# Last MLP of a hybrid attention block: its first two feature groups by pairs of row tiles

## The chip, the cores and the metric

The kernel runs on one core of a Trainium2 chip. The core has five engines that work side by side: TensorE (PE in the profile, its weight loads as PEld), VectorE (DVE), ScalarE (ACT), GpSimd (POOL) and SyncE (SP), which here only issues transfers. Each engine takes its own instructions strictly in the order in which they stand in its list and waits on semaphores for the others. Matmuls write to PSUM, everything else lives in SBUF, and inputs, outputs and some intermediate tensors in DRAM. The metric is the time of one launch in device microseconds.

## The reference

One transformer block over 1024 positions of width 1024 (float32): a hybrid attention, an attention to a memory of 256 rows, and an MLP with squared ReLU, each with a norm ahead and a residual add behind.

```python
x = x + hybrid_mixer(rms_norm(x, norm1_g), ...)          # sparse attention, 8 + 8 heads, @ w_out
x = x + memory_xattn(rms_norm(x, norm2_g), mem, ...)     # w_xq, 4 heads of 128 over 256 rows, @ w_xo
x = x + square(relu(rms_norm(x, norm3_g) @ w_ff_in)) @ w_ff_out   # 1024 -> 4096 -> 1024
```

## The kernel before

The 1024 rows are eight tiles of 128 (numbered 0 to 7). The kernel first projects all rows and runs the hybrid attention tile by tile. Beside the attention it runs a "filler": for tiles 0 to 3 the out projection, memory attention and whole MLP, then the out projection and memory attention of tiles 4 and 5. When the attention is over there remain the end of that filler, the same for tiles 6 and 7, and the MLP of tiles 4 to 7. This last part, from some 1330 us on, is what the change touches.

`between(pool, t0, nt, x2s, keep)` (L902) does the out projection and the memory attention for `nt` tiles from `t0`: it loads the attention outputs `o` (L908) and the residual `x` (L912), multiplies by `w_out` (fp32 matmuls of 256 columns, two TensorE passes each), adds to the residual (`add_to`, L899), norms (`norm_T2`, L290), multiplies by `w_xq`, and does one item of memory attention for each pair of heads and each tile (L939 to L986): scores, exponentials, transposes of the probabilities (L972), values; its output goes through DRAM (`xo`, written at L986, read at L992), is transposed and multiplied by `w_xo`. The result x2 stays in SBUF (`keep`) or goes to DRAM (L1000).

`mlp(pool, t0, nt, x2s)` (L1002) does the MLP of four tiles. It loads the x2 that are not in SBUF (L1007), norms and transposes all four tiles (each into a high and a low part, `xh` and `xl`, of fp32r type), then goes through eight groups of 512 features. In a group, four "feature" accumulations of 24 matmuls each (8 slices of k, times high-high, low-high, high-low) make 128 features for 512 rows: the weights are the stationary side, the 512 rows move. ScalarE takes relu and square (L1034, L1035), POOL splits the result into `h` parts (L1037, L1038). Then eight "down" accumulations (four tiles by two column halves) of 12 matmuls of 512 columns use the features as stationary side and `w_ff_out` as moving side; the DVE adds each to x2 (L899).

Every weight piece of 128 x 512 elements is loaded into `wraw` and split into a high and a low part (`split_w`, L240): the high part by ScalarE (L244), the low part by DVE or POOL (L249), as the list `plan["w"]` says in turn. `PLAN_TAIL` is ("ag", "av", "ag"): high always on ScalarE, low two times of three on POOL.

The order on each engine is not written out by hand. The program is traced in Python order (`merge` interleaves two generators by the weights they yield), and a planner then orders the instructions of each engine by the traced priority and by when, in its own model, their inputs and their buffers are ready. So work that is traced later is put into gaps where its inputs are there. A pool's tag is a ring of as many buffers as `RINGS` gives; a tile waits until the old user of its place is done. Transfers are issued in order by SP, and those of the memory's keys and values (L929, L930) by POOL.

The lines that set up the last part:

```python
merge((rest, REST), (between(d2, 6, 2, x2s, True), 45.0))
dn_pool.__exit__(None, None, None)
drain(mlp(d2, 4, 4, x2s))
```

`rest` is the remaining filler (memory attention of tiles 4 and 5, in pool `dn`); `d2` is the pool of the last part.

Of the kernel before, what the change touches and what calls it, by code (L numbers as in the profile page):

```python
# [10 lines left out]
F32R = mybir.dt.float32r  # L11
# [11 lines left out]
P = 128  # L23
L = 1024
DM = 1024
# [7 lines left out]
NCMP = 63  # L33
KG = 2
NS = 4
RINGS = {
    "p1": {"x4": 5, "st": 2, "relu": 4, "wraw": 4, "whi": 6, "wlo": 6, "c8": 4, "c4": 2, "kraw": 5, "pc": 2},
    "p2": {"x4": 3, "st": 1, "relu": 2, "whi": 4, "wlo": 4, "c8": 3, "c4": 1, "kraw": 4, "pc": 2},
    "dn": {"b4": 4, "h": 8, "relu": 2, "wraw": 2, "whi": 4, "wlo": 4},
    "d2": {"b4": 4, "h": 8, "relu": 2, "wraw": 3, "whi": 6, "wlo": 6},  # L40
}
PSUMS = {"p1": {"D": 4, "M": 3, "C": 1}, "main": {"S": 2, "PT": 2, "PV": 1, "D": 2, "M": 1}}
TAGS = {"p1": ("D", "M", "C"), "p2": ("D", "M", "D"), "dn": ("D", "M"), "d2": ("S", "PT")}
PLAN_HEAD = ("ag", "av")
PLAN_MAIN = ("ag",)
PLAN_TAIL = ("ag", "av", "ag")

SLC, WIN, DSA, IDX = 0, 2, 4, 5

# [34 lines left out]
def drain(gen):  # L84
    for _ in gen:
        pass
# [19 lines left out]
def merge(a, b):  # L106
    drain(beside(*a, *b))
# [59 lines left out]
def build(nc, tc, I, C, out):  # L167
# [72 lines left out]
    def split_w(raw, hi, lo):  # L240
        h, l = plan["w"][plan["i"] % len(plan["w"])]
        plan["i"] += 1
        if h == "a":
            s.activation(hi, raw, AF.Copy)  # L244
# [4 lines left out]
        (v if l == "v" else g).tensor_tensor(lo, raw, hi, op=ALU.subtract)  # L249
# [78 lines left out]
    def xT(pool, nt, whole=False):  # L328

        parts = [pool.tile([P, DM // P, nt * P], F32 if whole else F32R, tag="x" + n, name="x" + n)  # L330
                 for n in ("h" if whole else "hl")]
        return (parts, [lambda t, k, x=x: x[:, k, t * P:(t + 1) * P] for x in parts],
                lambda t: [x[:, :, t * P:(t + 1) * P] for x in parts])
# [565 lines left out]
            v.tensor_tensor(dst, pt, dst, op=ALU.add)  # L899
        return add_to  # L900

    def between(pool, t0, nt, x2s, keep):  # L902

        o_of = []
        for t in range(nt):
# [1 line left out]
            for c in range(8):  # L907
                nc.sync.dma_start(o[:, c, :], oT_dr[t0 + t][c])  # L908
            o_of.append(o)
        x2 = [ring(pool, "b4", [P, DM]) for t in range(nt)]  # L910
        for t in range(nt):
            nc.sync.dma_start(x2[t], I["x"][0, (t0 + t) * P:(t0 + t + 1) * P, :])  # L912
        add_to = residual_add(x2)
# [88 lines left out]
    def mlp(pool, t0, nt, x2s):  # L1002
# [13 lines left out]
        for f4 in range(8):  # L1016
# [24 lines left out]
            for c in range(2):  # L1041
# [4 lines left out]
                for t in range(nt):  # L1046
# [11 lines left out]
                                          x2[t][:, c * 512:(c + 1) * 512])  # L1058
                    yield 2.6

    def pe_stack():
# [68 lines left out]
    ctx.close()  # L1130


# [19 lines left out]
```

## Time and profile before

| | |
|---|---|
| median of 3 runs | 1837.35 us (1835.46 to 1839.35) |
| the profiled execution's own time | 1835.75 us |
| its span, first to last instruction | 1833.9 us |
| mean granted TensorE clock | 0.970 |
| TensorE busy | 1726.9 us (94%) |
| DVE, ACT, POOL busy | 936.1, 1074.6, 895.0 us |

The profile is of one execution. "Busy" is time in instructions of that engine. "Idle before" is an engine's waiting time just ahead of a group of instructions, with the engine or transfer that ended it. The granted clock is the share of full speed at which TensorE was let run. The chain is the sequence of work that ended last, followed back from the last instruction. A matmul's length in the profile includes its way through the pipeline, so the distance between the starts of two matmuls in a row is what one costs.

### The profile page before, as it was taken

Reading aid. Unit: us, or ns where it says so; the run is one execution under the profiler, and the core shown is the slowest. Engines: PE = TensorE matmul, PEld = TensorE weight load, DVE = VectorE, ACT = ScalarE, POOL = GpSimd, SP = SyncE. Lnnn points to the kernel's source line nnn. Section 1 sums busy time; section 2 is a strip of 40 time slices with the busy share of each in tenths; the row PEclk is TensorE's granted clock in tenths of the full one; section 3 lists DMA queues with packets and bytes.
Section 4 is the critical chain, followed back from the end, with each engine's and each line's share of the span. In section 5 each row is a group of like instructions: output and inputs, shape, how many; then the busy total and the mean of one; then the engine's idle time right before and its main releaser. Section 6 shows DMA issues by size and latency. Waiting matters only on the chain. (4 is left out here: it accounts for less than half of the span.)

```text
span 1833.9 us, 28049 instructions
## 1 busy us (share of the span) xinstructions
PE 1726.9 (94%) x9262; PEld 1474.2 (80%) x9262; DVE 936.1 (51%) x2353; ACT 1074.6 (59%) x2687; POOL 895.0 (49%) x1034
## 2 busy tenths in 40 slices
PE   5996999889989998999999999999999799999999
PEld 5995988777878787778887788888988578787787
DVE  4553766575684678466664656646523422222222
ACT  4444658889588669955797457994412323333332
POOL 2364657446262244677676576662111144454443
PEclk9997998999999999999999999999989799999999
DMA  8224512256335320222112112125394222222232
GB/s 203 70 87 160 103 34 79 78 193 180 122 112 162 120 81 24 73 81 71 64 63 91 54 65 75 60 79 185 99 288 131 71 69 92 92 93 93 94 99 98
DMA packets 180081, 187.50 MB, mean 102 GB/s; under 512 B 34656, under 2 KB 149088, under 8 KB 179936
## 3 DMA queue, kind: packets, MB, share of 16 engines
q1 hardware_dynamic: 172000, 175.23, 30.8%
q0 software_dynamic: 7936, 10.49, 2.2%
q8 instruction: 73, 1.20, 0.3%
q14 instruction: 72, 0.59, 0.1%
HBM read 164.69 MB, written 20.97 MB: 101 GB/s over the span
## 5 line engine op out<-in xcount | busy, mean ns | idle before, releaser
L249 POOL TENSOR_TENSOR wlo<-wraw,whi 128x512 fp32r<-128x512 f32 (+1 forms) x230 | 308.5, 1347 | 278.7 <-ACT whi L244 247.6
L244 ACT ACTIVATE whi<-wraw 128x512 fp32r<-128x512 f32 (+2 forms) x289 | 181.1, 628 | 247.4 <-PE psS L218 147.1
L218 PE MATMUL psD<-whi,xh 128*128 128x256 f32 (+1 forms) x704 | 193.8, 359 | 3.6 <-ACT whi L244 2.9
L218 PE MATMUL psD<-wlo,xh 128*128 128x256 f32 (+1 forms) x704 | 194.8, 357 | 0.8 <-DMA wlo<-in_w_in_dram 0.8
L236 DVE TENSOR_TENSOR pl<-psPT,ph 128x512 fp32r<-128x512 f32 (+1 forms) x232 | 142.2, 621 | 78.2 <-ACT ph L235 75.4
L218 PE MATMUL psD<-whi,h 128*128 128x512 f32 x512 | 174.3, 404 | 1.8 <-POOL h L1037 1.0
L688 ACT ACTIVATE S<-S,mn 128x128 f32<-128x128 f32 (+7 forms) x192 | 142.7, 744 | 41.5 <-DVE mn L686 40.3
L218 PE MATMUL psS<-whi,h 128*128 128x512 f32 x512 | 162.1, 392 | 5.1 <-DVE b L899 5.1
L693 POOL TENSOR_SCALAR S<-S,sums,gi 128x640 f32<-128x640 f32 (+7 forms) x128 | 107.7, 850 | 106.7 <-DVE sums L691 99.0
L235 ACT ACTIVATE ph<-psPT 128x512 fp32r<-128x512 f32 (+1 forms) x232 | 122.8, 540 | 60.9 <-PE psPT L703 54.5
L249 DVE TENSOR_TENSOR wlo<-wraw,whi 128x512 fp32r<-128x512 f32 (+1 forms) x59 | 64.3, 1090 | 166.9 <-ACT whi L244 166.8
L218 PEld LDWEIGHTS psD<-whi,xh 128*128 128x128 f32 x704 | 134.0, 198 | 14.3 <-ACT whi L244 3.3
L218 PEld LDWEIGHTS psD<-wlo,xh 128*128 128x128 f32 x704 | 134.8, 197 | 12.5 <-DMA wlo<-in_w_in_dram 1.2
L703 PE MATMUL psPT<-c_ident,S 128*128 128x128 f32 x816 | 132.3, 279 | 8.3 <-DVE ql L236 4.2
L899 DVE TENSOR_TENSOR b<-psS,b 128x512 f32<-128x512 f32 (+1 forms) x80 | 50.0, 635 | 152.6 <-PE psS L218 152.6
L218 PEld LDWEIGHTS psS<-whi,h 128*128 128x128 f32 x512 | 96.1, 188 | 29.3 <-DVE b L899 9.3
L218 PE MATMUL psS<-K,qh 128*128 128x384 f32 (+3 forms) x288 | 113.5, 397 | 5.6 <-DVE mn L686 2.8
L218 PEld LDWEIGHTS psD<-whi,h 128*128 128x128 f32 x512 | 95.6, 190 | 23.7 <-DVE b L899 1.5
L703 PEld LDWEIGHTS psPT<-c_ident,S 128*128 128x128 f32 x816 | 98.1, 143 | 18.9 <-POOL S L693 5.6
L218 PE MATMUL psD<-wlo,h 128*128 128x512 f32 x256 | 102.5, 404 | 1.3 <-POOL wlo L249 1.3
L218 PE MATMUL psD<-xh,wlo 128*128 128x512 f32 x256 | 101.5, 398 | 0.0
L899 DVE TENSOR_TENSOR b<-psD,b 128x512 f32<-128x512 f32 (+1 forms) x112 | 63.2, 572 | 74.5 <-PE psD L218 73.0
(299 smaller groups left out, 4647.4 us busy)
## 6 DMA issues: line engine op xcount, KB each, us to landing
wraw<-in_w_ff_in_dram SPq DMA_DIRECT2D x128, 256.0 KB, 2.7
wraw<-in_w_ff_out_dram SPq DMA_DIRECT2D x128, 256.0 KB, 2.6
whi<-in_w_out_dram SPq DMA_DIRECT2D x32, 256.0 KB, 5.0
wlo<-in_w_out_dram SPq DMA_DIRECT2D x32, 256.0 KB, 4.6
wraw<-in_w_in_dram SPq DMA_DIRECT2D x24, 256.0 KB, 3.1
q<-st SPq DMA_DIRECT2D x12, 512.0 KB, 2.6
qin<-q SPq DMA_DIRECT2D x44, 128.0 KB, 2.3
x<-in_x_dram SPq DMA_DIRECT2D x8, 512.0 KB, 5.2
```

Of the source, the lines that this page charges most:

```text
L218: te.matmul(o, a, b, start=start, stop=stop)
L235: s.activation(hi, src, AF.Copy)
L236: v.tensor_tensor(lo, src, hi, op=ALU.subtract)
L244: s.activation(hi, raw, AF.Copy)
L249: (v if l == "v" else g).tensor_tensor(lo, raw, hi, op=ALU.subtract)
L688: s.activation(S, S, AF.Exp, bias=low, scale=-1.0, accum_out=sums[:, hh:hh + 1])
L693: g.tensor_scalar(Ss[hh], Ss[hh], sums[:, hh:hh + 1], 1.0 if gate is None else gate[:, hh:hh + 1], op0=ALU.mult, op1=ALU.mult)
L703: te.transpose(p2[:, j, hh, :], S[:, (c + j) * P:(c + j + 1) * P], ident)
L899: v.tensor_tensor(dst, pt, dst, op=ALU.add)
```

## The change

The MLP of tiles 4 to 7 is written anew as `mlp_tail`. Its first `G` = 2 feature groups are done for tiles 4 and 5 alone, ahead (in traced order) of the norms of tiles 6 and 7; groups 2 to 7 are done for all four tiles; groups 0 and 1 for tiles 6 and 7 come last. The weights of groups 0 and 1 are therefore loaded and split twice. A feature accumulation of a pair has 256 rows in place of 512; down matmuls are as before. Weights come in chunks of 512 KB (four k slices of 256 columns, or two rows of 512) in place of 256 KB, and are split piece by piece as before.

The pools change with it. Residuals of the last part have a pool `res` of their own, norm weights a tag `g`, features a ring of 16 in place of 8. `d2` now only serves the memory attention of tiles 6 and 7, with weight rings of 4 in place of 6 and no `wraw`. The new pool `d3` lies on the side of `dn`, opens when `dn` and `d2` are closed, and takes its PSUM tiles from the tags D (two buffers) and M (one) in place of S and PT (two each). `PLAN_TAIL` alternates between POOL and DVE.

```diff
+G = 2
 RINGS = {
     "dn": {"b4": 4, "h": 8, "relu": 2, "wraw": 2, "whi": 4, "wlo": 4},
-    "d2": {"b4": 4, "h": 8, "relu": 2, "wraw": 3, "whi": 6, "wlo": 6},
+    "res": {"b4": 4},
+    "d2": {"b4": 2, "h": 8, "relu": 2, "whi": 4, "wlo": 4},
+    "d3": {"g": 2, "h": 16, "relu": 2, "wraw": 4, "whi": 10, "wlo": 10},
 }
-TAGS = {... "dn": ("D", "M"), "d2": ("S", "PT")}
+TAGS = {... "dn": ("D", "M"), "d2": ("S", "PT"), "d3": ("D", "M")}
-PLAN_TAIL = ("ag", "av", "ag")
+PLAN_TAIL = ("ag", "av")
...
-    def between(pool, t0, nt, x2s, keep):
+    def between(pool, t0, nt, x2s, keep, res=None):
...
-        x2 = [ring(pool, "b4", [P, DM]) for t in range(nt)]
+        x2 = [ring(res or pool, "b4", [P, DM]) for t in range(nt)]
...
+    def mlp_tail(pool, res, x2s, t0):
+        x2 = {}
+        (xh, xl), _, xt_of = xT(pool, 4)
+        gb3 = [ring(pool, "g", [P, 512]) for _ in range(2)]
+        for i, gb in enumerate(gb3):
+            nc.sync.dma_start(gb, row(W["norm3_g"][i * 512:(i + 1) * 512]).to_broadcast([P, 512]))
+
+        def start(t):
+            if t0 + t in x2s:
+                x2[t] = x2s[t0 + t]
+            else:
+                x2[t] = ring(res, "b4", [P, DM])
+                nc.sync.dma_start(x2[t], x2_dr[t0 + t])
+            norm_T2(pool, x2[t], gb3, xt_of(t))
+
+        def features(f4, ts):
+            cols = slice(ts[0] * P, (ts[-1] + 1) * P)
+            for f2 in range(2):
+                gr = []
+                for k0 in range(0, 8, 4):
+                    c0 = (f4 * 4 + f2 * 2) * P
+                    raw = ring(pool, "wraw", [P, 4, 256])
+                    nc.sync.dma_start(raw, W["w_ff_in"][k0 * P:(k0 + 4) * P, c0:c0 + 256]...)
+                    for k in range(0, 4, 2):
+                        hi, lo = ring(pool, "whi", [P, 2, 256], F32R), ring(pool, "wlo", [P, 2, 256], F32R)
+                        split_w(raw[:, k:k + 2, :], hi, lo)
+                        gr += [(hi[:, i, :], lo[:, i, :]) for i in range(2)]
+                for f in range(2):
+                    pt = pst(TAGS[pool.name][0], [P, len(ts) * P])
+                    fs = slice(f * P, (f + 1) * P)
+                    for k in range(8):
+                        wh, wl = gr[k]
+                        mm(pt, wh[:, fs], xh[:, k, cols], k == 0, False)
+                        mm(pt, wl[:, fs], xh[:, k, cols], False, False)
+                        mm(pt, wh[:, fs], xl[:, k, cols], False, k == 7)
+                    yield pt
+
+        def down(pt, hs, ws, us):
+            for f, ((hh, hl), (wh, wl)) in enumerate(zip(hs, ws)):
+                mm(pt, hh[:, us], wh, f == 0, False)
+                mm(pt, hh[:, us], wl, False, False)
+                mm(pt, hl[:, us], wh, False, f == len(hs) - 1)
+
+        def group(f4, ts, last):
+            hs = []
+            for pt in features(f4, ts):
+                n = len(ts) * P
+                r = ring(pool, "relu", [P, n])
+                s.activation(r, pt, AF.Relu)
+                s.activation(r, r, AF.Square)
+                hh, hl = ring(pool, "h", [P, n], F32R), ring(pool, "h", [P, n], F32R)
+                g.tensor_scalar(hh, r, 1.0, 1.0, op0=ALU.mult, op1=ALU.mult)
+                g.tensor_tensor(hl, r, hh, op=ALU.subtract)
+                hs.append((hh, hl))
+            for c in range(2):
+                cs = slice(c * 512, (c + 1) * 512)
+                ws = []
+                for k in range(0, 4, 2):
+                    raw = ring(pool, "wraw", [P, 2, 512])
+                    r0 = (f4 * 4 + k) * P
+                    nc.sync.dma_start(raw, W["w_ff_out"][r0:r0 + 256, cs]...)
+                    for i in range(2):
+                        hi, lo = ring(pool, "whi", [P, 512], F32R), ring(pool, "wlo", [P, 512], F32R)
+                        split_w(raw[:, i, :], hi, lo)
+                        ws.append((hi, lo))
+                for t in ts:
+                    pt = pst(TAGS[pool.name][0], [P, 512])
+                    down(pt, hs, ws, slice((t - ts[0]) * P, (t - ts[0] + 1) * P))
+                    v.tensor_tensor(x2[t][:, cs], pt, x2[t][:, cs], op=ALU.add)
+                    if last:
+                        nc.sync.dma_start(out[0, (t0 + t) * P:(t0 + t + 1) * P, cs], x2[t][:, cs])
+
+        for ts in ((0, 1), (2, 3)):
+            for t in ts:
+                start(t)
+            if ts[0] == 0:
+                for f4 in range(G):
+                    group(f4, ts, False)
+        for f4 in range(G, 8):
+            group(f4, (0, 1, 2, 3), False)
+        for t in (0, 1):
+            nc.sync.dma_start(out[0, (t0 + t) * P:(t0 + t + 1) * P, :], x2[t])
+        for f4 in range(G):
+            group(f4, (2, 3), f4 == G - 1)
...
-    d2_pool = tc.tile_pool(name="d2", bufs=1, side="right", reuse_waits="tile")
+    res_pool = tc.tile_pool(name="res", bufs=1, side="right", reuse_waits="tile")
+    res = res_pool.__enter__()
+    d2_pool = tc.tile_pool(name="d2", bufs=1, side="right", reuse_waits="tile")
...
-    merge((rest, REST), (between(d2, 6, 2, x2s, True), 45.0))
+    merge((rest, REST), (between(d2, 6, 2, x2s, True, res), 45.0))
     dn_pool.__exit__(None, None, None)
-    drain(mlp(d2, 4, 4, x2s))
     d2_pool.__exit__(None, None, None)
+    with tc.tile_pool(name="d3", bufs=1, reuse_waits="tile") as d3:
+        mlp_tail(d3, res, x2s, 4)
+    res_pool.__exit__(None, None, None)
     ctx.close()
```

More of the change, by code (lines that the diff above doesn't have):

```diff
@@ L39 @@
     "dn": {"b4": 4, "h": 8, "relu": 2, "wraw": 2, "whi": 4, "wlo": 4},
-    "d2": {"b4": 4, "h": 8, "relu": 2, "wraw": 3, "whi": 6, "wlo": 6},
+    "res": {"b4": 4},
+    "d2": {"b4": 2, "h": 8, "relu": 2, "whi": 4, "wlo": 4},
+    "d3": {"g": 2, "h": 16, "relu": 2, "wraw": 4, "whi": 10, "wlo": 10},
 }
 PSUMS = {"p1": {"D": 4, "M": 3, "C": 1}, "main": {"S": 2, "PT": 2, "PV": 1, "D": 2, "M": 1}}
-TAGS = {"p1": ("D", "M", "C"), "p2": ("D", "M", "D"), "dn": ("D", "M"), "d2": ("S", "PT")}
+TAGS = {"p1": ("D", "M", "C"), "p2": ("D", "M", "D"), "dn": ("D", "M"), "d2": ("S", "PT"), "d3": ("D", "M")}
 PLAN_HEAD = ("ag", "av")
 PLAN_MAIN = ("ag",)
-PLAN_TAIL = ("ag", "av", "ag")
+PLAN_TAIL = ("ag", "av")
 SLC, WIN, DSA, IDX = 0, 2, 4, 5
@@ L1059, in mlp @@
                     yield 2.6
+    def mlp_tail(pool, res, x2s, t0):
[18 more added lines that the diff above has]
+                    raw = ring(pool, "wraw", [P, 4, 256])
+                    nc.sync.dma_start(raw, W["w_ff_in"][k0 * P:(k0 + 4) * P, c0:c0 + 256].rearrange("(k p) n -> p k n", p=P))
+                    for k in range(0, 4, 2):
[33 more added lines that the diff above has]
+                    r0 = (f4 * 4 + k) * P
+                    nc.sync.dma_start(raw, W["w_ff_out"][r0:r0 + 256, cs].rearrange("(k p) n -> p k n", p=P))
+                    for i in range(2):
[20 more added lines that the diff above has]
+            group(f4, (2, 3), f4 == G - 1)
```

## The prediction

> **What bounds the kernel now.** I read the page's engine line and chain first, then the chain in order of time, then busy time in short windows around the place where the chain begins.
>
> The page, and the start and end of the chain in order of time (start, length, what):
>
> ```profile
> PE 1726.9 (94%) x9262; PEld 1474.2 (80%) x9262; DVE 936.1 (51%) x2353; ACT 1074.6 (59%) x2687; POOL 895.0 (49%) x1034
> PE 19%; DVE 1%; issue 0%
> ...
> 1469.14 28.00 PE psS L218 x119
> ...
> 1497.91 44.12 PE psS L218 x191
> ...
> 1542.05 0.70 DVE b L899
> ...
> 1542.80 44.12 PE psS L218 x191
> ...
> 1830.18 0.69 DVE b L899
> ```
>
> From 1469 us to the end the chain is TensorE alone: the last MLP, eight feature groups, each 1542.80 - 1497.91 = 44.89 us (192 matmuls and one wait of some 0.75 us for the DVE add that frees a PSUM tile). Nothing but fewer or denser TensorE instructions shortens that stretch. Ahead of it TensorE is not dense. Windows (length, then busy us and count of PE, PEld, DVE, ACT, POOL, granted clock, DMA share, GB/s):
>
> ```profile
> 1410.00:1420.00 10.00, 10.00 (x51) 8.91 (x51) 3.03 (x9) 1.15 (x3) 0.71 (x1) 1.00 0.62 199
> 1420.00:1430.00 10.00, 7.89 (x38) 5.91 (x37) 4.95 (x15) 4.92 (x14) 1.98 (x2) 0.78 0.47 157
> 1430.00:1440.00 10.00, 6.30 (x25) 5.39 (x25) 0.85 (x2) 0.60 (x1) 0.00 (x0) 0.50 0.27 80
> 1440.00:1450.00 10.00, 9.31 (x40) 7.69 (x39) 2.30 (x5) 1.86 (x3) 1.29 (x1) 0.86 0.09 26
> 1450.00:1460.00 10.00, 6.99 (x35) 5.53 (x33) 3.46 (x10) 5.14 (x10) 3.77 (x5) 0.99 0.25 79
> 1460.00:1470.00 10.00, 7.41 (x28) 5.36 (x28) 8.72 (x15) 5.06 (x9) 0.95 (x2) 0.50 0.00 0
> ```
>
> Between 1420 and 1470 TensorE works through the serial end of the memory attention of tiles 6 and 7, then the four norms, with gaps and a granted clock down to 0.50. All four norms come before the first feature matmul, so nothing fills these gaps. Its timeline there (start, length, instruction, idle before it and releaser):
>
> ```profile
> 1420.52 0.38 PE L274 MATMUL psPT<-c_ident,relu 128*128 128x128 f32 x2
> ...
> 1436.25 1.09 PE L274 MATMUL psPT<-c_ident,relu 128*128 128x128 f32 x4 [3.01 <-DMA relu<-xo]
> ...
> 1451.22 1.03 PE L218 MATMUL psS<-wlo,xh 128*128 128x256 f32 x4
> 1452.09 1.03 PE L218 MATMUL psS<-whi,xh 128*128 128x256 f32 x4
> ...
> 1458.68 1.34 PE L274 MATMUL psPT<-c_ident,relu 128*128 128x128 f32 x8 [2.98 <-DVE relu L297]
> ...
> 1468.79 0.78 PE L218 MATMUL psS<-xh,whi 128*128 128x512 f32 x1
> ...
> 1514.36 0.39 PE L218 MATMUL psS<-xh,whi 128*128 128x512 f32 x1
> ```
>
> The first feature matmul stands at 1468.79, the second group's first at 1514.36.
>
> **The change, part by part.** In the instruction order of the changed program every engine's list is the old one up to the start of the memory attention of tiles 6 and 7 (some 1330 us here); only what follows moves.
>
> *Feature groups 0 and 1 on tiles 4 and 5 alone.* They need only the norms of 4 and 5, so the planner lays their 2 x 96 feature and 2 x 48 down matmuls between the steps of the attention of 6 and 7, and the norms of 6 and 7 behind group 1. Groups 0 and 1 for tiles 6 and 7 come last. Feature matmuls are cut from 512 columns to 256, twice as many; down matmuls stay 512 wide and equal in number. The width's price is taken from the first projection, same type, same 256 columns:
>
> ```profile
> 30.00 0.28 PE L218 MATMUL psD<-whi,xl 128*128 128x256 f32 x1
> ...
> 31.81 0.28 PE L218 MATMUL psD<-wlo,xh 128*128 128x256 f32 x1
> ...
> 1475.24 0.39 PE L218 MATMUL psS<-xh,whi 128*128 128x512 f32 x1
> ...
> 1477.10 0.40 PE L218 MATMUL psS<-xl,whi 128*128 128x512 f32 x1
> ...
> 1513.46 0.62 PE L218 MATMUL psS<-whi,h 128*128 128x512 f32 x2
> ...
> 1514.14 0.39 PE L218 MATMUL psS<-whi,h 128*128 128x512 f32 x1
> ```
>
> Sixteen starts lie between the first two (all 17 are in the trace at 0.11 to 0.12): 1.81/16 = 0.113 us. At 512 columns the two rows stand eight starts apart: 1.86/8 = 0.232. Half of 0.232 is 0.116, so cutting the width costs nothing here: a pair's group is 96 x 0.114 + 48 x 0.227 (0.68/3) + 0.75 = 22.6 us, two of them 45.2 against 44.89. The wait for the DVE add comes once per pair instead of once per group, which is in the 45.2. The Trainium skill says otherwise (TensorE: Matmul & The Clock Gate, Back-to-back issue gap): pairs of weight load and matmul are said to sustain 81 ns at 128 columns and 131 at 512, which by a straight line, my estimate, puts 256 at three quarters of 512. By that rule the sum would rise by 384 x 0.25 x 0.232 = 22 us; the projection's rows do not agree with it.
>
> *What the filling can win.* In the old program the stretch 1420.5 to 1514.36 (93.9 us) holds group 0 and this work of 6 and 7 and of the norms, at full-clock prices: 64 passes of 0.217 us (0.87/4, above) = 13.9; 24 + 12 small attention matmuls at about 0.12 = 4.3; 52 transposes at about 0.12 = 6.2; together 24.4. With 45.2 for the pair groups that is 69.6: the ceiling of the gain is 93.9 - 69.6 = 24.3 us. The floor is below zero, since in-order queues can also make TensorE wait.
>
> *When the filling can start.* The x2 of tiles 4 and 5 still goes through DRAM. SP issues, and the first work released by the second read:
>
> ```profile
> 1415.13 0.32 SPq L1000 DMA_DIRECT2D x<-b  x1
> 1419.84 0.32 SPq L1007 DMA_DIRECT2D b<-x  x1
> 1422.49 0.69 POOL L231 TENSOR_TENSOR xqr<-xqms,mhalf 128x2 f32<-128x2 f32 x1 [0.38 <-DMA b<-x]
> L293 ACT ACTIVATE xh<-b 128x1024 fp32r<-128x1024 f32 x4 | 4.2, 1047 | 0.3 <-PE psS L218 0.3
> L244 ACT ACTIVATE whi<-wraw 128x512 fp32r<-128x512 f32 x13 | 8.2, 631 | 16.7 <-PE psS L218 16.3 <-issue 0.2
> L235 ACT ACTIVATE xh<-psPT 128x512 fp32r<-128x512 f32 x8 | 4.8, 596 | 5.1 <-PE psPT L274 5.1
> L966 ACT ACTIVATE relu<-psS,xnb,xsc 128x256 f32<-128x256 f32 x4 | 2.2, 562 | 1.4 <-DVE xnb L963 1.4
> L235 ACT ACTIVATE h<-psPT 128x256 fp32r<-128x256 f32 x2 | 0.8, 381 | 1.1 <-PE psPT L274 1.1
> ```
>
> Tile 5 lands at 1422.45. The changed order puts its sum of squares on ScalarE ahead of the query splits of 6 and 7, which now run as soon as their transposes (1420.52) are done: that chain starts late, at 1422.45 + 1.05 and a short read of the sum, about 1423.7. Before the norm of 5 is split (its first half), ScalarE's list holds two query splits, both halves of 4, six weight splits and two exponentials: 2 x 0.38 + 3 x 0.60 + 6 x 0.63 + 2 x 0.56 = 7.5, so 1431.2; with a DVE subtraction, the second half's transposes and handoffs dense features run from about 1434.5. TensorE has 14 us from 1420.5 to there and 4.9 us of work in it (16 norm and 9 other transposes, 12 score matmuls, four features, at 0.12): 9.1 lost. The first weights come late as well: the old program had three chunks loaded long before, now the first load stands behind tile 5's read on SP (1419.84 + 0.32); the read itself took 2.6 us to land, and twice that for the larger chunk still hides behind the same wait.
>
> *Interleaving.* DVE and POOL now split weights (32 pieces for the two pair groups) while the attention of 6 and 7 needs them. Group rows of the dense MLP, and one DVE split with POOL idle:
>
> ```profile
> L249 POOL TENSOR_TENSOR wlo<-wraw,whi 128x512 fp32r<-128x512 f32 x48 | 63.9, 1339 | 83.3 <-ACT whi L244 82.7
> L249 DVE TENSOR_TENSOR wlo<-wraw,whi 128x512 fp32r<-128x512 f32 x24 | 27.2, 1131 | 81.9 <-ACT whi L244 81.9
> 1474.47 0.69 DVE L249 TENSOR_TENSOR wlo<-wraw,whi 128x512 fp32r<-128x512 f32 x1 [3.98 <-ACT whi L244]
> ```
>
> A split takes DVE 1.13 on average against 0.69 alone. I take 3 us for small waits of this kind and 1.5 for the low clock at the start (0.50 in two of the windows). The bounds are 0 and 21: the two returns of the attention output through DRAM, priced below, hidden or bare; 3 is near the lower end since each has some 8 us of matmuls in front. The Trainium skill (SBUF — State Buffer, two separate sides) names an exclusive port pair for which the loser of DVE and POOL waits through the other's whole instruction; the 1.13 agrees, and by it a DVE step of the attention could wait up to a POOL split longer.
>
> *Other queues and pools.* SP loses the three early loads; residuals with their own pool are read before the attention outputs, two issues (0.3 to 0.5 us each) off the way to w_out. The d2 weight rings fall from 6 to 4, so w_out's third chunk waits for its first: at worst a landing (2.6 us, as above) lies bare, though a chunk of w_out is 32 passes, 6.9 us, of cover. I set the two against each other: 0, bounds -1 and +2. At the end each pair group splits its 16 pieces in 22.6 us: on POOL eight low parts, and four feature splits of two 256-wide instructions, each under 1.34: at most 16 x 1.34 = 21.4 us, so it holds. DVE now takes half of the low parts instead of a third: 8 x 1.13 in 44.89, hidden.
>
> **Sum.** 69.6 + 9.1 + 3 + 1.5 puts the end of group 1 and of the attention at 1420.5 + 83.2 = 1503.7 against 1514.36: -10.7. The last two pair groups, 45.2 against 44.89, give +0.3: -10.4. The span of 1833.9 becomes 1823.5, the profiled execution's 1835.75 becomes 1825.3. That execution is 1.6 under the median of 1837.35; against the median I put 1826.9.
>
> **Rivals.**
> *The filling fits without friction.* The attention chain of 6 and 7 would be hidden from 1424 on, and only x2's landing is lost, 4 us: gain 19, time 1817. For it: TensorE is 10.00 busy in the window before 1420, where two such streams are already interleaved. Against: the queue of ScalarE above.
> *The groups do not start early.* The new pool lies over that of tiles 4 and 5 and its tiles wait for the old ones; if these waits, or late weights, hold features until the attention is done (1444 to 1455), most of the gap stays: 1833 to 1837. Against: the loads go out at 1420.
> *SP holds the attention back (slower).* In the new order the write and read of the attention output of tile 6 stand behind the fifth and sixth weight loads, those of tile 7 behind the eighth, and these wait for slots that DVE and POOL free. The return alone costs:
>
> ```profile
> 1433.74 0.42 SPq L986 DMA_DIRECT2D xo<-relu  x1
> 1436.57 0.32 SPq L992 DMA_DIRECT2D relu<-xo  x1
> 1441.60 1.06 PE L274 MATMUL psPT<-c_ident,relu 128*128 128x128 f32 x4
> ```
>
> That is 7.9 us from write to transposes. TensorE is in order: two returns, each with two splits (2 x 1.34) in front, bare, would be 21 us, 18 above what I took, so 1845. The gain is gone once 13.4 of the 21 lie bare. Against: 60 features and 12 small matmuls (8.2 us) stand in front of the first return's transposes, 48 features and nine down matmuls (7.5) in front of the second's.
> *Narrow matmuls cost more.* If 256 columns took 0.217 as the fp32 passes do, 384 x 0.10 = 38 us more, 1865. The projection's rows speak against it. By the Trainium skill's rule above it would be 22 us more.
>
> **How the numbers follow.** The forecast as worked out (1820 to 1833) has 0.55; the frictionless case 0.2; no early start 0.12; SP 0.1; narrow matmuls 0.03. A measurement here tells about 0.2% (3.7 us) from no change. Faster holds the first two, 0.75, and a little of the third: 0.78. Same is most of the third and some of the fourth, 0.11; slower 0.11. The range reaches from the frictionless case and some 3 us past it (the prices at 0.12 are rounded), 1814, into the case without early start, 1836.
>
> **What would show it.** In the changed trace: 256-wide feature matmuls 0.114 apart from about 1434; group 2's first 512-wide one near 1504; six periods of about 44.9 us, then two of about 22.6; TensorE idle of some 9 us between 1420 and 1435 and under 5 us between 1435 and 1500; a granted clock of 1.00 from 1440. It is wrong if TensorE waits for the return of the attention output by more than 10 us, if 256-wide starts are further apart than 0.13, or if the last pair groups wait for weights.

## The result and the profile after

The changed kernel takes 1826.46 us (median of four runs, 1821.91 to 1827.33) against 1837.31 for the kernel before: a ratio of 0.9935, 95% interval 0.9918 to 0.9952, so 9 to 15 us less against a measurement that tells some 4. The prediction was 1826.9. The profiled execution is the fastest of the four (1821.91 us, span 1820.1), while that of before was a middling one. The page of the changed kernel:

```profile
PE 1715.2 (94%) x9454; PEld 1475.6 (81%) x9454; DVE 957.4 (53%) x2390; ACT 1094.6 (60%) x2735; POOL 910.1 (50%) x1045
```

The total hides where the time went, so I cut the span at four instructions that both kernels have, in TensorE's timeline (start, length, instruction, idle before it and releaser). Before:

```profile
1334.99 4.94 PE L218 MATMUL psD<-h 128*128 128x128 f32 x22
...
1785.10 0.39 PE L218 MATMUL psS<-xh,whi 128*128 128x512 f32 x1
...
1829.76 0.39 PE L218 MATMUL psS<-whi,h 128*128 128x512 f32 x1
```

After:

```profile
1330.51 4.11 PE L221 MATMUL psD<-h 128*128 128x128 f32 x22
...
1412.35 0.38 PE L277 MATMUL psPT<-c_ident,relu 128*128 128x128 f32 x2
...
1500.28 0.51 PE L221 MATMUL psD<-xh,whi 128*128 128x512 f32 x1 [0.83 <-ACT xh L238]
...
1768.90 0.28 PE L221 MATMUL psD<-xh,whi 128*128 128x256 f32 x1
...
1815.83 0.39 PE L221 MATMUL psD<-whi,h 128*128 128x512 f32 x1
```

The first row (a values product of the memory attention of tiles 4 and 5) is the last instruction whose whole past on the four computing engines is the same in both programs (SP already issues other transfers before it). The second is the last query transposes of tile 6 (those of tile 7 follow at 1421.99 and 1415.62); the matmul records between the two (430 after, 429 before) are of the same kinds in both programs, in a slightly different order. The third is the first 512-wide feature matmul behind the interleaved stretch (group 2's after, group 1's before), the fourth stands six whole groups later. Before, the second and third are the rows at 1420.52 and 1514.36 of the prediction.

| stage, us | before | after | difference | forecast |
|---|---|---|---|---|
| A: values product to query transposes | 85.53 | 81.84 | -3.69 | 0 |
| B: query transposes to the first 512-wide group | 93.84 | 87.93 | -5.91 | -10.7 |
| C: six whole groups | 270.74 | 268.62 | -2.12 | 0 |
| D: the rest, to the last matmul | 44.66 | 46.93 | +2.27 | +0.3 |
| tail, A to D | 494.77 | 485.32 | -9.45 | -10.4 |

The first row itself stands 4.5 us earlier in the profile after, which the change cannot have done; over all profiled executions below it stands anywhere from 1330.5 to 1336.0. So each kernel below is told by its time and by its tail.

Stage B in windows (length, busy us and count of PE, granted clock, DMA share, GB/s):

```profile
1412.35:1426.59 14.24, 7.63 (x34) 0.67 1.01 332
1426.59:1434.00 7.41, 7.41 (x47) 0.71 0.55 164
1434.00:1484.60 50.60, 50.60 (x317) 1.00 0.44 136
1484.60:1500.28 15.68, 11.05 (x44) 0.78 0.35 112
```

Between 1434 and 1485 the gap is filled: TensorE is busy throughout at full clock. The stage is 87.93 long for the 69.6 of work that the prediction counted, so 18.3 are lost where 13.6 were forecast. With the prediction's prices (estimates, rounded, so that they sum to 19), some 10 go in the first window, 2 in the second to the low clock, and 7 in the last. Of these 7, 4.6 are waits (3.80 and 0.83, below and above); most of the rest is the clock, which is at 0.50 again around the longer wait. TensorE works in 5.31 of these 6.80 us, at half speed, which costs some 2.7:

```profile
1488.90:1495.70 6.80, 5.31 (x15) 0.50 0.38 130
```

The timeline of TensorE in the middle and in the last window:

```profile
1442.06 0.60 PE L277 MATMUL psPT<-c_ident,relu 128*128 128x128 f32 x4
...
1445.98 0.60 PE L277 MATMUL psPT<-c_ident,relu 128*128 128x128 f32 x4
...
1484.61 0.60 PE L277 MATMUL psM<-c_ident,relu 128*128 128x128 f32 x4
...
1490.39 1.09 PE L277 MATMUL psM<-c_ident,relu 128*128 128x128 f32 x4 [3.80 <-DVE xl L239]
```

The first two are the returns of the attention output of tiles 6 and 7 through DRAM: no idle before them, so the feared wait is hidden. The loss of the last window is one that the prediction has no line for: the norm of tile 6 has one PSUM tile (tag M); its second half can be transposed only when the DVE has read the first, and the DVE's list shows why that is late:

```profile
1482.34 2.58 DVE L252 TENSOR_TENSOR wlo<-wraw,whi 128x512 fp32r<-128x512 f32 x2
1485.55 2.43 DVE L300 SCALAR_TENSOR_TENSOR relu<-b,nr,g 128x512 f32<-128x512 f32 x2 [0.63 <-POOL h L1118]
1487.90 1.75 DVE L252 TENSOR_TENSOR wlo<-wraw,whi 128x512 fp32r<-128x512 f32 x1
1489.57 0.68 DVE L239 TENSOR_TENSOR xl<-psM,xh 128x512 fp32r<-128x512 f32 x1
```

The weight split of 1.75 just ahead of the read runs beside one on POOL (1487.34 to 1489.10); alone it takes 0.68 to 0.69 (19 splits of this kernel from 1400 us on that no POOL instruction overlaps).

### The profile page after: what moved, and what is told of

The parts are those of the page before. It is cut to its first block, busy times and chain, and to the rows that moved or that the text cites. A ratio compares the mean times of both kernels' runs of the same rounds, so it can differ in the third digit from the quotient of the medians.

```text
span 1820.1 us, 28417 instructions
## 1 busy us (share of the span) xinstructions
PE 1715.2 (94%) x9454; PEld 1475.6 (81%) x9454; DVE 957.4 (53%) x2390; ACT 1094.6 (60%) x2735; POOL 910.1 (50%) x1045
## 3 DMA queue, kind: packets, MB, share of 16 engines
q8 instruction: 75, 1.23, 0.3%
## 4 chain that ended last, share of the span: by engine, by line
PE 66%; DVE 9%; ACT 8%; POOL 7%; issue 5%; DMA 5%; SPq 0%; POOLq 0%; ACTq 0%; DVEq 0%
PE psD L221 47%; PE psS L221 8%; PE psPV L221 4%; PE psPT L706 4%; ACT dmask L647 2%; POOL wlo L252 2%; PE psM L277 1%; POOL S L696 1%; DMA wraw<-in_w_ff_in_dram 1%; DVE S L689 1%; DVE pl L239 1%; ACT whi L247 1%; ACT ph L238 1%; ACT tkt L649 1%; ACT tks L648 1%
## 5 line engine op out<-in xcount | busy, mean ns | idle before, releaser
L221 PE MATMUL psD<-whi,h 128*128 128x512 f32 x1024 | 340.7, 401 | 7.3 <-DVE b L1134 5.4
L247 ACT ACTIVATE whi<-wraw 128x512 fp32r<-128x512 f32 x321 | 200.7, 628 | 209.9 <-PE psD L221 155.1
L221 PEld LDWEIGHTS psD<-whi,h 128*128 128x128 f32 x1024 | 192.9, 190 | 53.1 <-DVE b L1134 8.8
L221 PE MATMUL psD<-xh,wlo 128*128 128x512 f32 (+1 forms) x576 | 212.7, 370 | 0.0
L221 PE MATMUL psD<-xh,whi 128*128 128x512 f32 (+1 forms) x576 | 211.8, 372 | 0.9 <-ACT xh L238 0.8
L221 PE MATMUL psD<-xl,whi 128*128 128x512 f32 (+1 forms) x576 | 212.2, 370 | 0.0
L221 PE MATMUL psD<-wlo,h 128*128 128x512 f32 x512 | 203.3, 399 | 1.3 <-POOL wlo L252 1.3
L221 PEld LDWEIGHTS psD<-whi,xh 128*128 128x128 f32 x704 | 132.3, 195 | 14.2 <-ACT whi L247 3.4
L221 PEld LDWEIGHTS psD<-xh,whi 128*128 128x128 f32 x576 | 108.8, 189 | 18.6 <-ACT xh L238 1.6
L221 PEld LDWEIGHTS psD<-xh,wlo 128*128 128x128 f32 x576 | 108.9, 189 | 17.1 <-POOL wlo L252 0.3
L221 PEld LDWEIGHTS psD<-xl,whi 128*128 128x128 f32 x576 | 108.8, 189 | 17.1
```

The costliest lines, as they stand in the source:

```text
L221: te.matmul(o, a, b, start=start, stop=stop)
```

## The experiments

Stages of each kernel as above, in us; the kernel before had medians of 1835.4 to 1837.3 in these comparisons.

| kernel | time | ratio to before, 95% | A | B | C | D | tail |
|---|---|---|---|---|---|---|---|
| before | | | 85.5 | 93.8 | 270.7 | 44.7 | 494.8 |
| changed | 1826.5 | 0.9935 (0.9918 to 0.9952) | 81.8 | 87.9 | 268.6 | 46.9 | 485.3 |
| whole groups | 1834.5 | 0.9990 (0.9979 to 1.0002) | 82.6 | 100.2 | 268.0 | 44.5 | 495.3 |
| before, x first | 1836.8 | 1.0005 (0.9993 to 1.0018) | 86.7 | 94.4 | 270.9 | 44.7 | 496.7 |
| before, x first, rings of 4 | 1847.8 | 1.0068 (1.0044 to 1.0092) | 88.6 | 95.9 | 278.2 | 46.5 | 509.2 |
| changed, x late, rings of 6 | 1828.2 | 0.9956 (0.9941 to 0.9970) | 87.9 | 86.8 | 268.5 | 46.9 | 490.2 |
| changed, norms in PT | 1830.7 | 0.9967 (0.9955 to 0.9979) | 82.4 | 96.6 | 268.1 | 46.9 | 494.0 |
| changed, x2 kept | 1825.9 | 0.9939 (0.9927 to 0.9951) | 83.2 | 86.6 | 268.6 | 46.9 | 485.3 |
| changed, low on DVE | 1819.7 | 0.9908 (0.9892 to 0.9925) | 81.6 | 80.9 | 269.0 | 46.1 | 477.6 |
| changed, low on POOL | 1834.2 | 0.9998 (0.9989 to 1.0007) | 81.8 | 90.8 | 269.7 | 54.0 | 496.3 |
| changed, low on DVE, x2 kept | 1813.7 | 0.9878 (0.9859 to 0.9897) | 83.0 | 79.3 | 269.0 | 46.1 | 477.5 |
| changed, three pairs | 1826.8 | 0.9953 (0.9938 to 0.9969) | 82.7 | | | | 489.5 |
| changed, three pairs, low on DVE | 1819.8 | 0.9913 (0.9897 to 0.9929) | 82.6 | | | | 480.5 |
| before, low on DVE | 1834.0 | 0.9992 (0.9979 to 1.0005) | 85.2 | 94.7 | 269.5 | 44.7 | 494.1 |

With x2 kept, the first four norm transposes of tile 4 stand in stage A instead of B.

### Are the pair groups the gain?

```diff
-G = 2
+G = 0
...
-            group(f4, (0, 1, 2, 3), False)
-        for t in (0, 1):
+            group(f4, (0, 1, 2, 3), G == 0 and f4 == 7)
+        for t in (0, 1) if G else ():
```

> The changed kernel with all eight feature groups done for all four tiles (G = 0): pools, PSUM tags, load sizes and the early read of the residual stay as changed, only the pair groups are gone. Theory of the prediction: pools and queues are worth nothing and the pair groups 10.4 us, so this runs like the kernel before, 1837 us (1835 to 1839), and the stage from the first values matmul psD<-h of tiles 4 and 5 (1334.99 before) to the query transposes of 6 and 7 (1420.52) stays at 85.5 us. Rival: that stage became 3.7 us shorter by the rearrangement (1330.51 to 1412.35, 81.8 us, in the changed kernel), so this keeps about 3.7 us of the gain, 1833.6 us, with 82 us for the stage, and the pair groups are worth only some 7 us.

Measured: 1834.5 us, stage A 82.6, tail 495.3. Both theories are half right. The pools do shorten stage A, which the prediction had at nothing, and what stays of it in the end is hardly told from no change, because stage B grew from 93.8 to 100.2: the new MLP without pair groups puts its norms, with one PSUM tile, and its weight splits into the old gap:

```profile
1460.73 0.66 PE L277 MATMUL psM<-c_ident,relu 128*128 128x128 f32 x4 [1.64 <-DVE relu L300]
1463.62 0.90 PE L277 MATMUL psM<-c_ident,relu 128*128 128x128 f32 x4 [2.23 <-DVE xl L239]
1466.06 1.08 PE L277 MATMUL psM<-c_ident,relu 128*128 128x128 f32 x4 [1.54 <-DVE xl L239]
```

The pair groups take that stage to 87.9, so they are worth 12.2 in it and cost 2.5 in stage D: with everything, 9.9 of the tail and 8.1 of the medians.

### What shortened stage A?

Three edits of the kernel touch it: x read early (into a pool of its own, `res`), rings of 4 for 6, no MLP loads beside the attention. First, x alone, in the kernel before, but into `d2`:

```diff
-    def between(pool, t0, nt, x2s, keep):
+    def between(pool, t0, nt, x2s, keep, res=None):
+        if res:
+            x2 = [ring(res, "b4", [P, DM]) for t in range(nt)]
+            for t in range(nt):
+                nc.sync.dma_start(x2[t], I["x"][0, (t0 + t) * P:(t0 + t + 1) * P, :])
         o_of = []
...
-        x2 = [ring(pool, "b4", [P, DM]) for t in range(nt)]
-        for t in range(nt):
-            nc.sync.dma_start(x2[t], I["x"][0, (t0 + t) * P:(t0 + t + 1) * P, :])
+        if not res:
+            x2 = [ring(pool, "b4", [P, DM]) for t in range(nt)]
...
-    merge((rest, REST), (between(d2, 6, 2, x2s, True), 45.0))
+    merge((rest, REST), (between(d2, 6, 2, x2s, True, d2), 45.0))
```

> The kernel before with one edit: in the out projection of tiles 6 and 7 the residual x is read before the sixteen pieces of the attention output instead of after them. Theory of the prediction: worth 0, 1837 us, stage (values matmul to query transposes) 85.5 us. Rival A: the two reads of x (512 KB each) ahead of the first out-projection weights on the queue were what TensorE waited for at 1349 and after, so the stage falls to about 82 us and the time to 1833.6. Rival B: the 3.7 us come from the loads that the changed kernel no longer makes there (early MLP weights, rings of 6), so the stage stays at 85.5 here.

Then with the smaller rings:

```diff
-    "d2": {"b4": 4, "h": 8, "relu": 2, "wraw": 3, "whi": 6, "wlo": 6},
+    "d2": {"b4": 4, "h": 8, "relu": 2, "wraw": 3, "whi": 4, "wlo": 4},
```

> The kernel before with the residual x read ahead of the attention output and the weight rings of the last part cut from 6 to 4, as in the changed kernel; MLP and early MLP loads as before. Only the stage from the first values matmul to the query transposes of 6 and 7 is read (85.5 us before, 81.8 changed, 82.6 with whole groups, 86.7 with x first alone). Theory: the shallower ring paces the weight loads, so that fewer of them stand in the queue and on the DMA engines ahead of the returns of the attention output: 82 to 83.5 us. Rival: it is the early loads of MLP weights and norm weights, which are still here: 85 to 87 us. The dense groups may be slower for the smaller ring.

Then the changed kernel with x late and rings of 6, so that only the MLP loads are gone:

```diff
-    "res": {"b4": 4},
-    "d2": {"b4": 2, "h": 8, "relu": 2, "whi": 4, "wlo": 4},
+    "d2": {"b4": 6, "h": 8, "relu": 2, "whi": 6, "wlo": 6},
...
-    merge((rest, REST), (between(d2, 6, 2, x2s, True, res), 45.0))
+    merge((rest, REST), (between(d2, 6, 2, x2s, True, d2), 45.0))
...
+        mlp_tail(d3, d2, x2s, 4)
```

> The changed kernel with the pools of the memory attention as before: rings of 6, the residual x read after the attention output, from the same pool; only the MLP's own pool, and with it the absence of MLP loads in that stage, stays. Read in the stage from the first values matmul to the query transposes of 6 and 7 (85.5 us before; 86.7 with x first; 88.6 with x first and rings of 4; 81.6 to 83.2 in all kernels with the MLP in its own pool). Theory: the early MLP loads ahead of the last out-projection weights and the returns of the attention output are what cost 3 us, so the stage is 82 to 84 us here and the time 1826 to 1828. Rival: only the three edits together do it, and the stage goes back to 85 us or more, the time to 1829 to 1831.

Measured: 86.7, 88.6 and 87.9, all above the 85.5 of before, while the seven kernels of the table with the changed pools and no kept x2 stand at 81.6 to 82.7. So neither this form of x first does it, nor x with the rings, nor the missing MLP loads alone. That only the three together do it, the rival of the last run, is not shown by this: its stage came out, but its time of 1828.2 lies between the two ranges, and the rings alone, or the missing loads with one of the others, were not run. Nor is x first the changed kernel's edit. There the reads go into the pool `res`, and SP issues the two 8.5 us ahead of the values product; from `d2` they go out 3.3 us ahead of it, straight in front of the attention output. SP's timeline of the changed kernel, then of x first:

```profile
1321.99 0.93 SPq L915 DMA_DIRECT2D b<-in_x_dram  x2
```

```profile
1328.67 1.02 SPq L907 DMA_DIRECT2D b<-in_x_dram  x2
```

All nine kernels with `res` issue x 8.5 to 8.9 us ahead, and they are the nine with the shorter stage; so the early read from a pool of its own is a rival that none of these runs tests.

What can be seen: before, the first `w_out` matmul stands 14.5 us behind the values product, in the changed kernel 12.1. With x first it stands at 12.8, so up to there rival A has its way, and the gain is lost further on: both of the waits for transfers that the kernel before has in stage A are still there (1.15 and 1.36), and one of 1.02 for the DVE has come. Timeline of before:

```profile
1349.51 1.97 PE L218 MATMUL psS<-whi,b 128*128 128x256 f32 x8 [0.67 <-DMA whi<-in_w_out_dram]
...
1394.59 0.63 PE L274 MATMUL psM<-c_ident,relu 128*128 128x128 f32 x4 [1.16 <-DMA relu<-xo]
```

The changed kernel has neither wait; the two are 1.8 of the 3.7 us. Some 1.0 more is the clock: the granted clock of the stage is 0.95 before and 0.96 after, and length times the missing share gives 4.3 and 3.3 us (estimates). In the last run it is 0.92, or 7.0 us, so some of its 87.9 is clock too. By which path the edits shorten this stage stays open.

### Is it the single PSUM tile?

```diff
-TAGS = {... "d3": ("D", "M")}
+TAGS = {... "d3": ("D", "PT")}
```

> The changed kernel with the transposes of the last MLP's norms in PSUM tag PT (two buffers) instead of M (one). Theory: the 3.80 us for which TensorE waits at 1490.39 for the DVE's low part of tile 6, the 0.83 at 1500.28 and part of the low clock that follows are the single buffer's; with two, the second half of tile 6 is transposed at once, and the time falls by 3 to 5 us to 1821.5 to 1823.5. Rival: the norm of tile 6 is late because the DVE does weight splits ahead of its scalings (2.58 and 1.75 us each at 1482 to 1489), so the wait only moves to the scaled rows, and the time stays within 1.5 us of 1826.5.

Measured: 1830.7 us, stage B 96.6: neither. Sharing PT with the memory attention put the norms of tiles 4 and 5 behind the return of the attention output, and the pair groups with them:

```profile
1436.13 1.08 PE L277 MATMUL psPT<-c_ident,relu 128*128 128x128 f32 x4 [5.60 <-DMA relu<-xo]
...
1450.29 0.47 PE L221 MATMUL psD<-xh,whi 128*128 128x256 f32 x1
```

Features start at 1450 instead of 1426.6. This is the prediction's rival of no early start, by another road. Even so tile 6 waits 0.86 for a scaled row and 2.30 for its low part at the end of group 1, so two buffers do not remove that wait. What two buffers that nothing else uses would be worth, this run does not show.

### Is it the landing of x2?

```diff
+    late = {}
...
-            dst = x2[t][:, ci * w:(ci + 1) * w]
-            v.tensor_tensor(dst, pt, dst, op=ALU.add)
+            src = x2[t][:, ci * w:(ci + 1) * w]
+            dst = src
+            if to is not None:
+                if t not in to:
+                    to[t] = ring(late["res"], "b4", [P, DM])
+                dst = to[t][:, ci * w:(ci + 1) * w]
+            v.tensor_tensor(dst, pt, src, op=ALU.add)
...
-        yield from between(dn, 4, 2, {}, False)
+        yield from between(dn, 4, 2, late, "res")
...
+        x2s.update((t, late[t]) for t in (4, 5))
```

> The changed kernel with the x2 of tiles 4 and 5 kept in SBUF: the adds of their last product write straight into the residual pool, and the write to DRAM and the read back are gone. Theory: the read of tile 5 (issued 1408.79, landed 1415.31, 6.5 us) sets the start of the first features, so they start 5 to 8 us earlier (at about 1420 instead of 1426.6) and the time falls by 4 to 7 us, to 1819.5 to 1822.5. Rival: ScalarE's list (query splits, halves of the norms, weight splits, exponentials) and the first weight loads set the start, so the features move by less than 2 us and the time stays at 1824.5 to 1827.

Measured: 1825.9 us, tail 485.3, the changed kernel's own. The chain of the changed kernel goes through that landing,

```profile
1408.79 6.52 DMA b<-x
```

yet without it the first feature stands at 1425.94, 0.65 earlier. The rival's size holds, but hardly by ScalarE's list as it says: ahead of the last two halves of the norms ScalarE itself is idle, 1.79 and 2.79 us, until TensorE has transposed them. What the trace shows instead is that the weight splits, now loaded even earlier, run on DVE and POOL ahead of the attention's and the norm's own steps. The DVE's timeline of the kernel with x2 kept, then POOL's:

```profile
1415.50 1.75 DVE L300 SCALAR_TENSOR_TENSOR relu<-b,nr,g 128x512 f32<-128x512 f32 x1
```

```profile
1413.62 4.76 POOL L252 TENSOR_TENSOR wlo<-wraw,whi 128x512 fp32r<-128x512 f32 x3 [1.50 <-ACT whi L247]
1419.15 0.69 POOL L234 TENSOR_TENSOR xqr<-xqms,mhalf 128x2 f32<-128x2 f32 x1 [0.77 <-DVE xqms L232]
```

A scaling of a half row takes 1.75 instead of 0.74 while POOL splits. That led to the next runs.

### Are DVE and POOL in each other's way?

```diff
-PLAN_TAIL = ("ag", "av")
+PLAN_TAIL = ("av",)
```

> The changed kernel with every low part of a weight split on DVE (PLAN_TAIL of one entry, high on ScalarE, low on DVE). Theory P: in the handoff and at the norm of tile 6 the DVE is slow because POOL splits beside it (1.77 and 1.79 us for a split at 1418 and 1421, against 0.68 alone); with POOL out of it a split costs 0.69, features start 2 to 4 us earlier than 1426.6, the 3.80 us wait for tile 6 shrinks below 1, and the time falls to 1820 to 1823. Rival Q: what counts is how many splits stand ahead of the norm steps on the in-order DVE; there are twice as many now, so the waits stay or grow and the time is 1826 to 1831.

Measured: 1819.7 us, stage B 80.9: theory P. With twice as many splits on the DVE, each of them got shorter. Groups of the DVE from 1405 to 1500 (busy, mean ns of one), of the changed kernel and then of this one:

```profile
L252 DVE TENSOR_TENSOR wlo<-wraw,whi 128x512 fp32r<-128x512 f32 x21 | 21.1, 1003 | 16.0 <-ACT whi L247 16.0
L300 DVE SCALAR_TENSOR_TENSOR relu<-b,nr,g 128x512 f32<-128x512 f32 x8 | 7.9, 1010 | 2.0 <-POOL h L1118 1.3 <-DMA g<-in_norm_g_dram 0.6
```

```profile
L252 DVE TENSOR_TENSOR wlo<-wraw,whi 128x512 fp32r<-128x512 f32 x42 | 29.6, 727 | 11.3 <-ACT whi L247 11.2
L300 DVE SCALAR_TENSOR_TENSOR relu<-b,nr,g 128x512 f32<-128x512 f32 x8 | 5.9, 745 | 1.4 <-DMA g<-in_norm_g_dram 0.7 <-POOL h L1118 0.6
```

42 splits cost the DVE 8.5 us more than 21, and POOL is spared 21 of 1.4 each. In TensorE's timeline the wait of tile 6 goes from 3.80 to 1.23:

```profile
1491.10 0.63 PE L277 MATMUL psM<-c_ident,relu 128*128 128x128 f32 x4 [1.23 <-DVE xl L239]
```

Two parts of the expectation failed: that wait is not below 1, and the features start 13.3 us behind the query transposes, against 14.2, not 2 to 4 earlier. So 6.1 of the 7.0 us that stage B loses lie later in it. The waits there fall from 4.6 to 2.0 (1.23 and 0.77). Most of the rest is the clock: it stays at 1.00 where the changed kernel had 0.50 (window as above, last part of the stage):

```profile
1485.40:1498.54 13.14, 11.15 (x54) 1.00 0.55 164
```

This goes through all profiles with pair groups: six have a wait of 2.30 to 3.80 us at the norm of tile 6 and around it or just behind it 6.8 to 6.9 us at a clock of 0.50; the three with all low parts on DVE have waits of 1.23 to 1.24 and none. So in these kernels the collision is paid twice, as a wait and as low clock.

The opposite:

```diff
-PLAN_TAIL = ("ag", "av")
+PLAN_TAIL = ("ag",)
```

> The changed kernel with every low part of a weight split on POOL. DVE has no splits at all: theory Q then expects the 3.80 us wait for tile 6 to go and the features to start earlier. But a pair group needs 16 splits of 1.34 us and 8 instructions for the features on POOL, 21.4 + some 5 = 27 us in a group of 22.6, so the pair groups become POOL's: four times some 4 us, less what is saved, 1832 to 1840. Rival: the early pair groups run beside the attention and have room, and only the last two pay: 1826 to 1832.

Measured: 1834.2 us, stage D 54.0. The last two pair groups take 29.4 and some 25 us and wait for POOL's feature splits (three waits, 3.8 us, in the first of them). The wait of tile 6 does not go either (3.65, for its scaled row). With no split on the DVE, the scaling first waits for a buffer that POOL has to free, and then takes 5.27 us instead of 0.74, beside five POOL instructions in a row. The DVE's timeline, then POOL's:

```profile
1485.68 5.27 DVE L300 SCALAR_TENSOR_TENSOR relu<-b,nr,g 128x512 f32<-128x512 f32 x1 [14.88 <-POOL h L1118]
```

```profile
1485.59 0.43 POOL L1117 TENSOR_SCALAR h<-relu 128x256 fp32r<-128x256 f32 x1
1485.96 2.54 POOL L252 TENSOR_TENSOR wlo<-wraw,whi 128x512 fp32r<-128x512 f32 x2
1488.43 0.76 POOL L1118 TENSOR_TENSOR h<-relu,h 128x256 fp32r<-128x256 f32 x1
1489.11 1.29 POOL L252 TENSOR_TENSOR wlo<-wraw,whi 128x512 fp32r<-128x512 f32 x1
```

The scaling ends 0.55 us behind the last of them.

The last one puts the plan of low parts on DVE into the kernel before:

```diff
-PLAN_TAIL = ("ag", "av", "ag")
+PLAN_TAIL = ("av",)
```

> The kernel before with every low part of the last MLP on DVE, nothing else. Theory: what the DVE splits gain is gained where splits stand between the steps of a serial chain; in the kernel before the chain of 6 and 7 has none beside it and the dense groups have room, so little moves: 1834 to 1838. Rival: it is a gain of its own, in the dense groups or the norms, and the kernel before gets 5 us or more of it: 1828 to 1831.

Measured: 1834.0 us, tail 494.1: as the theory says, little; the interval includes no change. In these kernels the collision costs time where splits run between the steps of a serial chain.

### With both, and with more pairs

Low parts on DVE and x2 kept (the two diffs above):

> The changed kernel with every low part on DVE and the x2 of tiles 4 and 5 kept in SBUF. Kept alone moved nothing (1825.9 against 1826.5), low parts on DVE alone gave 1819.7. Theory: with the splits out of the way the landing of tile 5 is what the start of the features waits for (ScalarE idle 2.3 us for it, sum of squares behind it), so that now keeping it helps: 1815 to 1818. Rival: the exponentials and query splits of 6 and 7 set the start in any case: 1819 to 1821.

Measured: 1813.7 us, the fastest of all and below both ranges; its interval just touches that of low on DVE alone. But the trace does not show where: the tail is 477.5 against 477.6 with x2 through DRAM, and the 3 us by which this profiled execution is faster lie before the values product, in work that is the same. (It is also the slowest of this kernel's five.) The features start 9.8 us behind the query transposes instead of 13.3, but four transposes of that work now lie ahead of the cut, and stage A is longer. Counted from the values product they start 2.0 us earlier, and of this 0.3 is left where the second pair group starts. The median speaks for the theory, the trace for the rival; open.

Three pair groups (G = 3), with the changed plan and with low parts on DVE:

> The changed kernel with three groups by pairs (G = 3). Theory: the gaps that pair groups can fill are used up by two of them; what a third adds is its own price, by the rows of the changed kernel 1.1 us for each pair group (the last two took 46.93 us against 44.66 for one whole group), so 1827.5 to 1829. Rival: 18.3 us of the stretch from 1412.35 to 1500.28 are still lost, and more early work fills part of them: 1822 to 1825.

> The changed kernel with every low part on DVE and three groups by pairs. Theory: two pair groups fill what can be filled, a third costs its own price; with low parts on DVE the last pair groups took 46.1 us against 44.7 for one whole group, so 0.7 each, 1.4 for two more: 1820.5 to 1822. Rival: as with G = 3 and the old split, nothing is lost within a us: 1819 to 1820.

Measured: 1826.8 and 1819.8 us, within half a us of the medians with two pairs; the tails are longer by 4.2 and 2.9, of which 0.9 and 1.0 lie in stage A. The first median lies between the two ranges, the second in its rival's; the tails lose somewhat more than the first theory says. So more pairs fill nothing more, since the loss lies at the two ends of the gap and not in it, and whether the third pair costs anything the medians don't tell.

## Why the prediction was right

The time is right to 0.4 us, the tail to 1.0 (-9.45 against -10.4), and the mechanism is shown: without the pair groups nearly all of the gain is gone. But four terms were off, by 2 to 5 us each, and they cancelled; that the sum came out to 0.4 us is luck.

*What bounds the kernel, and the ceiling.* Right: the gap was filled, from 1434 to 1485 without idle time, the six whole groups follow, and the two pair groups at the end.

*Narrow matmuls.* Right: in the pair groups at the end 192 feature matmuls take 22.62 us, 0.118 each, under the bound of 0.13. The rival of dear narrow matmuls is out, and with it, for these matmuls, the reading of the Trainium skill (TensorE: Matmul & The Clock Gate, Back-to-back issue gap) that I had set against the row.

*The handoff.* Its size was right (9.1 lost forecast, some 10 measured; features first at 14.2 us behind the query transposes, 14 forecast for dense ones), its cause was not: the step said that the landing of tile 5 sets it, and without that landing the features moved by 0.65. The landing was misread as well: 2.6 us was taken from a POOL instruction (`xqr<-xqms`) that does not read x2. The profile of before has 3.4 us from issue to landing for that read, and the changed kernel 6.5.

*Interleaving.* Too small: 3 of waits plus 1.5 for the clock forecast, some 9 measured: 4.6 of waits and, at half speed under work, some 4.8 of clock (2.1 at the start, 2.7 at the norm of tile 6, where the prediction had put the clock at 1.00). The step looked for the loss at the returns of the attention output, where there is none (the rival of SP is out), and not at the norm of tile 6, which the same change puts behind the weight splits of groups 1 and 2 with one PSUM tile. The clue stood in the step itself: a split costs the DVE 1.13 on average beside POOL and 0.69 alone. I priced that as small waits. The run with low parts on DVE takes 7.0 off the stage, 0.9 of it in the handoff. The Trainium skill (SBUF — State Buffer, two separate sides) says that the one of DVE and POOL that comes second is fully blocked for the other's instruction; the split of 1.75 at 1487.90, which ends 0.55 behind the POOL split begun before it, agrees. The scaling of 5.27 was held longer than one instruction, through five. The Trainium skill (Perfetto Trace Analysis, Optimizing Scalar/DVE Operations) warns that moving work between those two might not help; here sharing cost more than giving all of it to the DVE (1826.5 against 1819.7 us), and all on POOL most (1834.2).

*Pools and queues.* Set to 0, bounds -1 and +2; measured -3.7 in stage A, outside the bounds, some 1.0 of it clock. The step priced the early read of x by SP's two issues (0.3 to 0.5 us each) alone; before, the two reads land at 1346.2 and 1348.2 and the first chunk of `w_out` behind them at 1349.4, and x first brings the first `w_out` matmul 1.7 us forward. What makes up the rest stays open.

*Whole groups.* Set to 0, measured -2.1 over six. They come every 44.65 to 45.24 us against 44.89, and two of the old six had a second wait for the DVE add, at 45.6. No run takes this apart.

*The end.* +0.3 forecast, +2.3 measured. The list of POOL held, as forecast; the DVE's did not: an add stands behind a split of the new plan, in TensorE's timeline:

```profile
1787.37 0.50 PE L221 MATMUL psD<-whi,h 128*128 128x512 f32 x1 [1.51 <-DVE b L1134]
```

With low parts on DVE the wait is 0.69 and the stage 46.1.

Sum: -3.7 and -2.1 not forecast, +4.8 in stage B and +2.0 at the end not forecast: +1.0. One rival was mis-added: by its own terms (24.3 - 4 - 0.3) the frictionless case gains 20, not 19; the 1817 beside it is right.

## What to carry to other kernels

Two engines that slow each other must be priced as one queue: when splits of weights are moved beside a serial chain, count how long each step of the chain becomes while the other engine works, and try giving all of it to one engine. A long transfer on the chain is not yet worth its length; take it away and see whether the next wait stands right behind it. When a total agrees, cut both traces at the same instructions: here a forecast right to 1 us held four terms that were off by 2 to 5.

## What the runs showed of the hardware that I had not expected

A DVE split that reads two SBUF tensors took 0.68 to 0.69 us alone and up to 1.79 where a POOL instruction overlapped it, and doing twice as many of them with POOL's splits out of the way took less than one and a half times as long (29.6 against 21.1). A DVE scaling of 0.74 took 5.27 us while five POOL instructions followed each other without a gap. A TensorE wait of 2.30 to 3.80 us came with 6.8 to 6.9 us at a granted clock of 0.50 in six profiles, one of 1.23 to 1.24 with none in three. Work that is the same instruction by instruction scatters by 5.5 us over 1330 us between executions, more than several of the effects measured here.
